# Storing split weight blocks of the input projection for their later uses, in a hybrid decoder layer

## The chip, the cores and the metric

The kernel runs on one core of a Trainium2 chip. The metric is device time in microseconds (us) of one execution; it is the median of several runs, 1899.0 us before the change. Five engines work side by side, each on its own queue in order: TensorE (PE; its weight loads are listed apart as PEld), VectorE (DVE), ScalarE (ACT), GpSimd (POOL) and SyncE (SP), which here issues nearly all transfers between HBM and the on-chip memory (SBUF). TensorE writes into PSUM banks.

## The reference

One decoder layer, 2048 tokens, width 1024, all in float32:

```
hn  = RMSNorm(x)
[u | q | k | v] = hn @ W_in          # W_in: 1024 x 2048, four parts of 512 columns
y_pool = per group of 128 columns: (mean of the last w tokens - own value) @ pool_w, times pool_scale   # w = 2, 4, 8, 16
y_attn = strictly causal stick-breaking attention, 8 heads of 64
h = x + concat(RMSNorm(y_pool), RMSNorm(y_attn)) @ W_out
h = h + relu(RMSNorm(h) @ W_up)**2 @ W_down
y = RMSNorm(h)
```

## The kernel before, in words

*Number format.* Every float32 operand of a large product is split into a high part (rounded to the type float32r) and a low part (the rest). A product is three matmuls: high by high, high by low, low by high. The split is the helper `split`: ScalarE copies the high part (line 145), VectorE subtracts it from the source (line 146). These two lines thus carry the splits of many tiles, and the tile names in the profile tell them apart: `hl` is a weight granule, `h` a normalised activation, `qk` and `vt` query, key and value tiles, `at` the attention weights, `pls` a pooled tile, `mix` a normalised mixer output.

*Tiling.* The 2048 tokens are four token blocks of 512 (j = 0 to 3). W_in is 16 column blocks of 128 (0 to 3 pool groups, 4 to 7 queries, 8 to 11 keys, 12 to 15 values). One block of W_in against one token block is a step: 8 chunks of the inner dimension, each three matmuls of 128 x 512 (lines 177, 178, 179), 24 in all, into one PSUM tile `pd`.

*Weights.* A column block is loaded raw (`load_raw`, line 159, 512 KB, two buffers `raw`), and split into two granules of four chunks each (`weights`). A granule `hl` holds its high and low parts, 512 KB in all. Five buffers `hl` rotate (WAHEAD = 5): a granule's buffer is free when TensorE has done the matmuls of the granule five back. `weights` is called ahead of each step and readies granules up to five ahead of it.

*Order of the steps.* `front(0)` runs ten steps of token block 0 (blocks 4, 8, 5, 9, 12, 13 and then pool groups 0 to 3), then a shared stage in which blocks 6, 10, 14, 7, 11, 15 are each split once and used for token blocks 0 and 1, then the ten blocks of token block 1. `front(1)` does the same for token blocks 2 and 3. The ten blocks that are not shared are thus loaded and split four times each, once per token block. In the trace the stages lie at 0 to 67 us (token block 0), 67 to 162 (shared, 0 and 1), 162 to 238 (token block 1), 238 to 318 (token block 2), 318 to 413 (shared, 2 and 3) and 413 to 494 (token block 3). Then come 32 steps with W_out (`tail`, to 692 us), and the feed-forward part to the end.

*Work around the steps.* After a step its PSUM tile is evacuated: `keep_qk` splits queries and keys and stores them to HBM, `keep_v` does so for values over a transpose (`ptv`), `pool_group` forms the pooled tile (`pl`), splits it (`pls`) and multiplies it by pool_w into `pp` (lines 396 to 398). The attention of earlier tokens (`near`) is a generator of pieces put between the steps by due times (`advance`, RATIO_FRONT). Norms are pieces in a list `later`, taken one or two per step (`catch_up`). `inv_rms` makes a root chain: sums of squares by matmuls into `pm` (line 204), a first VectorE step (line 212), ten and more small GpSimd steps, then matmuls into `pr` (line 230) that spread the result, which ScalarE copies (line 250). At the start of the last stage `load_mix` (line 547) brings the mixer's tiles `h<-mx` for W_out.

*Queues.* The program states an order and some constraints (`issue_after`): among them, `catch_up` (line 1491) holds the pieces in `later` behind the newest weight split on ScalarE's or VectorE's queue (`last_split`), and `load_x` (line 304) holds the loads of x behind the newest raw load (`last_load`). The order on each engine's queue is then chosen by a planner that simulates the times of all instructions. Each queue, SP's too, runs in the order chosen: an instruction that waits holds up those behind it.

*Names.* The change touches `load_raw`, `weights`, `start`, `in_proj`, the list `wlist` of column blocks in the order of their first use, and the call for W_out in `tail`. It uses the lists EARLY (4, 8, 12, 5, 9, 13) and POOL (0, 1, 2, 3).

Of the kernel before, what the change touches and what calls it, by code (L numbers as in the profile page):

```python
# [8 lines left out]
F32 = mybir.dt.float32  # L9
F32R = mybir.dt.float32r  # L10
# [5 lines left out]
P = 128  # L16
# [9 lines left out]
G = 4  # L26
# [15 lines left out]
POOL, EARLY, FIRST = (0, 1, 2, 3), (4, 8, 12, 5, 9, 13), (4, 8, 5, 9, 12, 13)  # L42
# [3 lines left out]
def hymba_block(ctx: ExitStack, tc: tile.TileContext, xT, gains, w_in, pool_w, w_out, w_up, w_down, out):  # L46
    nc = tc.nc
# [5 lines left out]
    dram = pool("dram", 1, space=bass.MemoryType.DRAM)  # L53
# [76 lines left out]
    os_ = [dram.tile([H // 2, P, T], F32, name=f"os{j}") for j in range(NT)]  # L130
    mx = [[dram.tile([P, 2, T], F32R, name=f"mx{j}_{k}") for k in range(KD)] for j in range(NT)]
    hs = [dram.tile([KD, P, T], F32, name=f"hs{j}") for j in range(NT)]

    su = [[[dram.tile([P, 2, T], F32, name=f"su{q}_{i}_{c}") for c in range(2)] for i in range(7)] for q in range(2)]
    sd = [[[dram.tile([P, 2, T], F32, name=f"sd{q}_{i}_{c}") for c in range(8)] for i in range(7)] for q in range(2)]
# [6 lines left out]
    def split(dst, src):  # L142

        hi, lo = dst
        nc.scalar.activation(hi, src, AF.Copy)  # L145
        return nc.vector.tensor_tensor(lo, src, hi.bitcast(F32), ALU.subtract)  # L146
# [6 lines left out]
    raws, grans, last_split, last_mm, last_load = [], [], [None], [None], [None]  # L153
    done = [None, None]

    def load_raw(i):
        while len(raws) <= min(i, len(wlist) - 1):
            raw = wp.tile([P, 2, G, P], F32, tag="raw", name="raw")
            last_load[0] = nc.sync.dma_start(raw, wlist[len(raws)].rearrange("p (x k) c -> p x k c", x=2))
            raws.append(raw)  # L160

    def weights(first, n):

        for i in range(len(grans), min(first + WAHEAD, 2 * len(wlist))):
            load_raw(i // 2)
            hl = wp.tile([P, 2, G, P], F32R, tag="hl", name="hl", align_bytes=256, bufs=WAHEAD)
            last_split[0] = split((hl[:, 0], hl[:, 1]), raws[i // 2][:, i % 2])
            grans.append(hl)
            load_raw(i // 2 + 1)
        return grans[first:first + n]  # L170

    def products(ps, hls, acts, half_behind=None):
# [112 lines left out]


    wlist = []
    prog = []

    def step(n, emit, again=False):  # L290
        prog.append((n, emit, again))
# [15 lines left out]
    def start():  # L307

        xt = st[0]["x"] = x0p.tile([P, KD, T], F32, tag="big", name="xt")
        for _ in range(2):  # L310
            raws.append(wp.tile([P, 2, G, P], F32, tag="raw", name="raw"))
        def weight(c, x):
            nc.sync.dma_start(raws[c][:, x], wlist[c][:, x * G:(x + 1) * G])

        nc.scalar.dma_start(xt[:, 0], xT[0, :, 0])
        weight(0, 0)
        nc.sync.dma_start(gt, gains)
        weight(1, 0)
        for k in range(1, KD):
            if k == 3:  # L320
                weight(0, 1)
            if k == 4:
                weight(1, 1)
            nc.sync.dma_start(xt[:, k], xT[0, :, k])

        zb = zero.bitcast(BF16)
        pz = psx.tile([P, T], F32, tag="px", name="pzero")
        for i in range(WARM):
            nc.tensor.matmul(pz, zb[:, 0:P], zb[:, 0:T], start=True, stop=True)
# [41 lines left out]
    def pool_group(j, g, ps):  # L371
        w = WINDOWS[g]
        if g == 0:
            st[j]["y"] = pa.tile([P, 4, T], F32, tag="yb", name="yb", bufs=1)
        u = pa.tile([P, PAD + T], F32, tag="u", name="u")
        nc.gpsimd.tensor_copy(u[:, 0:PAD], carry[:, g])
        if j == 0:
            took = nc.vector.tensor_tensor(u[:, PAD:], ps, st[0]["r"], ALU.mult)
        else:
            took = nc.scalar.activation(u[:, PAD:], ps, AF.Copy)  # L380
        nc.gpsimd.tensor_copy(carry[:, g], u[:, T:T + PAD])
        cur, lag = u, 1
        while lag < w:
            nxt = pa.tile([P, PAD + T], F32, tag="s", name="s")
            lo = 2 * lag - 1
            nc.vector.tensor_tensor(nxt[:, lo:], cur[:, lo:], cur[:, lo - lag:PAD + T - lag], ALU.add)
            cur, lag = nxt, 2 * lag
        pl = pa.tile([P, T], F32, tag="ev", name="pl")
        nc.vector.scalar_tensor_tensor(pl, cur[:, PAD:], 1.0 / w, u[:, PAD:], op0=ALU.mult, op1=ALU.subtract)
        if j == 0:  # L390
            nc.vector.tensor_tensor(pl[:, 0:w - 1], cur[:, PAD:PAD + w - 1], recip[:, 0:w - 1], ALU.mult)
            nc.vector.tensor_tensor(pl[:, 0:w - 1], pl[:, 0:w - 1], u[:, PAD:PAD + w - 1], ALU.subtract)
        d = pa.tile([P, 2, T], F32R, tag="st", name="pls", align_bytes=256, bufs=3)
        split((d[:, 0], d[:, 1]), pl)
        pp = psx.tile([P, T], F32, tag="px", name="pp")
        nc.tensor.matmul(pp, pw[0][:, 0, g], d[:, 0], start=True, stop=False)
        nc.tensor.matmul(pp, pw[0][:, 0, g], d[:, 1], start=False, stop=False)
        nc.tensor.matmul(pp, pw[0][:, 1, g], d[:, 0], start=False, stop=True)
        nc.scalar.activation(st[j]["y"][:, g], pp, AF.Copy, scale=gs[:, g:g + 1])
        return took  # L400
# [46 lines left out]

    def in_proj(j, c, again=False):
        if not again:
            wlist.append(w_in[c])  # L450
        if c < 4:
            evac = lambda ps: pool_group(j, c, ps)
        elif c < 12:
            evac = lambda ps: keep_qk(j, c % 4, qs if c < 8 else ks, ps)
        else:
            evac = lambda ps: keep_v(j, c - 12, ps)
        n = sum(1 for _ in prog if _[0]) if j == 0 else None

        def emit(w):
            dense(j, "h", w, evac, None, "pm" if n == 2 else None)  # L460

        def emit_two(w):

            ps = [psd.tile([P, T], F32, tag="pd", name="pd") for _ in range(2)]
            for k, (hi, lo) in enumerate(st[0]["h"]):
                for i in range(2):
                    hl, c = w[2 * i + k // G], k % G
                    nc.tensor.matmul(ps[i], hl[:, 0, c], hi, start=(k == 0), stop=False)
                    nc.tensor.matmul(ps[i], hl[:, 0, c], lo, start=False, stop=False)
                    last_mm[0] = nc.tensor.matmul(ps[i], hl[:, 1, c], hi, start=False, stop=(k == KD - 1))  # L470
            for i in range(2):
                done[:] = [done[1], pending[i](ps[i])]

        if n is not None and len(pending) < 2:
            pending.append(evac)
            if len(pending) == 2:
                step(4, emit_two)
            return
        step(2, emit, again)
# [9 lines left out]
    def drained(j):  # L489
        while j not in finished:  # L490
            state["due"] = 0.0
            advance(0.1)
# [62 lines left out]
    def tail(first):  # L555

        def root(j):

            if not (first and j < 2):
                drained(j)  # L560
                st[j]["todo"] = attn_norm(j, lambda: make_h(j))

        def mixes(j):
            load_mix(j, KD if first and j < 2 else 4)
            if "todo" in st[j]:
                st[j]["amix"] = st[j].pop("todo")()

        def begin(j):
            catch_up(len(later))
            st[j]["m"] += st[j].pop("amix", [])  # L570
            if j > 0:
                norm2(j - 1)
            if j == 2:
                sums_first()

        if first:
            note(to_out)
        else:
            note(lambda: (root(0), mixes(0), load_acc(0)))
        for j in range(NT):  # L580
            if j == 2 and first:
                note(to_last)
            note(lambda j=j: begin(j))
            for c in range(KD):
                if c == 0 and j == 0 and not first:
                    note(lambda: root(1))
                if c == 0 and j + 1 < NT:
                    note(lambda j=j: mixes(j + 1))
                if c == (2 if j == 0 else 4) and j + 2 < NT:
                    note(lambda j=j: root(j + 2))  # L590
                if c == 0 and j == 2:
                    note(lambda j=j: load_acc(j))
                if c == 4 and j in (0, 2):
                    note(lambda j=j: load_acc(j + 1))
                if c == 3 and j == NT - 1:
                    note(begin_ffn)
                wlist.append(w_out[c])
                step(2, lambda w, j=j, c=c: dense(j, "m", w, lambda ps: add_acc(j, c, ps)))


# [1042 lines left out]
```

## Time and profile before

| | us |
|---|---|
| runs shown | 1898.85, 1899.0, 1906.92 (median 1899.0) |
| profiled execution, its own time | 1905.2 |
| its span, first to last instruction | 1903.5 |
| TensorE busy | 1869.5 |
| VectorE busy | 1480.9 |
| ScalarE busy | 1023.7 |
| weight splits, 168: ScalarE, VectorE | 104.2, 113.9 |
| bytes moved | 535.91 MB, mean 282 GB/s |

A row that names an engine, a line and `out<-in` is a group of equal instructions; after `|` stand their busy time and the mean time of one in ns, then the idle time of the engine ahead of them with what ended most of it. A row that begins with a stretch (from:to, in us from the span's start) gives the stretch's length, each engine's busy time in it with its count of instructions, the clock granted to TensorE as a share, the share of time for which the 16 DMA engines were busy, and GB/s. A row `A <- B` gives who waited for whom: us in all, how often, the longest. TensorE's matmuls overlap, so busy time counts a matmul until its modelled end.

### The profile page before, as it was taken

What the parts mean: (1) busy time and instruction counts of PE and PEld (TensorE: products, weight loads), DVE (VectorE), ACT (ScalarE), POOL (GpSimd) and SP (SyncE); (2) the same over time, 40 slices, a digit from 0 to 9 for tenths busy, and PEclk for the clock granted to TensorE, in tenths of its full rate; (3) what the DMA queues carried; (4) which work ended last, traced back from release to release, by engine and by line L of the source; (5) the groups of instructions that cost most, each with busy time, mean ns of one, the idle gap of its engine ahead of it and who ended that gap; (6) DMA issues with size and microseconds to landing.
All of it is one profiled execution on the core that took longest, in us unless ns stands there. A gap on an engine that the chain in (4) does not pass through costs nothing.

```text
span 1903.5 us, 26682 instructions
## 1 busy us (share of the span) xinstructions
PE 1869.5 (98%) x8883; PEld 1555.5 (82%) x8883; DVE 1480.9 (78%) x2151; ACT 1023.7 (54%) x1616; POOL 242.1 (13%) x463
## 2 busy tenths in 40 slices
PE   9999999999999999999999999999999999999997
PEld 7888788888888888778888888887788888888886
DVE  6887799668866976778699988786566677888774
ACT  5565466555544465554557555554332665656543
POOL 0333233223421050000000000000010010020120
PEclk9999999999999999999999999999999999999998
DMA  6686696798788867887899888889999899999752
GB/s 224 204 269 196 191 308 213 239 322 278 272 316 306 296 229 254 284 306 276 286 365 334 313 300 278 301 284 326 378 311 326 289 322 301 334 297 342 290 210 91
DMA packets 222164, 535.91 MB, mean 282 GB/s; under 512 B 26048, under 2 KB 32192, under 8 KB 218176
## 3 DMA queue, kind: packets, MB, share of 16 engines
q1 hardware_dynamic: 217264, 525.46, 79.2%
q0 software_dynamic: 4608, 8.39, 2.4%
q8 instruction: 72, 1.18, 0.3%
q14 instruction: 76, 0.62, 0.1%
q10 hardware_dynamic: 144, 0.26, 0.0%
HBM read 349.46 MB, written 184.55 MB: 281 GB/s over the span
## 4 chain that ended last, share of the span: by engine, by line
PE 45%; DMA 6%; DVE 4%; issue 2%; ACT 1%; POOL 0%; SPq 0%; DVEq 0%; ACTq 0%
PE pb L1274 14%; PE pb L1451 12%; PE pY L1101 10%; PE pZ L1101 5%; PE pX L1101 2%; DMA ar<-sd 1%; DVE hw L146 1%; DMA ar<-sdi 1%; PE pb L1391 1%; DMA t<-in_w_down_dram 1%; DMA su<-hs 0%; DMA sd<-a 0%; DMA td<-t 0%; DMA sdi<-a 0%; DMA b<-in_w_down_dram 0%
## 5 line engine op out<-in xcount | busy, mean ns | idle before, releaser
L1101 PE MATMUL pY<-sa,hw 128*128 128x512 f32 x1536 | 366.3, 389 | 3.0 <-ACT u L1024 2.6
L1101 PEld LDWEIGHTS pY<-sa,hw 128*128 128x128 f32 x1536 | 288.0, 188 | 64.3 <-ACT u L1024 3.9
L1274 PE MATMUL pb<-ad,wd 128*128 128x512 f32 x1344 | 305.1, 389 | 0.3 <-DVE ad L146 0.3
L177 PE MATMUL pd<-h,hl 128*128 128x512 f32 x752 | 299.0, 398 | 3.5 <-DVE acc L813 2.0
L179 PE MATMUL pd<-h,hl 128*128 128x512 f32 x752 | 297.6, 396 | 0.0
L178 PE MATMUL pd<-h,hl 128*128 128x512 f32 x752 | 297.5, 396 | 0.0
L1274 PEld LDWEIGHTS pb<-ad,wd 128*128 128x128 f32 x1344 | 252.2, 188 | 53.1 <-DVE ad L146 0.7
L1451 PE MATMUL pb<-ad,wd 128*128 128x512 f32 x1104 | 253.9, 390 | 2.4 <-ACT ad L145 2.0
L1451 PEld LDWEIGHTS pb<-ad,wd 128*128 128x128 f32 x1104 | 206.5, 188 | 46.1 <-ACT ad L145 2.4
L146 DVE TENSOR_TENSOR ad<-ar,ad 128x1024 fp32r<-128x1024 f32 x160 | 193.9, 1220 | 44.6 <-ACT ad L145 44.2
L145 ACT ACTIVATE ad<-ar 128x1024 fp32r<-128x1024 f32 x160 | 168.2, 1053 | 95.2 <-PE pb L1451 32.0
L1101 PE MATMUL pZ<-sa,hw 128*128 128x512 f32 x768 | 187.0, 390 | 1.1 <-DVE a L1044 1.0
L1101 PEld LDWEIGHTS pZ<-sa,hw 128*128 128x128 f32 x768 | 143.7, 188 | 32.4 <-DVE a L1044 2.6
L177 PEld LDWEIGHTS pd<-h,hl 128*128 128x128 f32 x752 | 142.6, 190 | 31.8 <-issue 2.8
L145 ACT ACTIVATE hl<-raw 128x512 fp32r<-128x512 f32 x168 | 104.2, 631 | 116.2 <-PE pd L179 66.1
L179 PEld LDWEIGHTS pd<-h,hl 128*128 128x128 f32 x752 | 142.5, 189 | 28.2
L178 PEld LDWEIGHTS pd<-h,hl 128*128 128x128 f32 x752 | 142.5, 190 | 26.8
L146 DVE TENSOR_TENSOR hl<-raw,hl 128x512 fp32r<-128x512 f32 x168 | 113.9, 684 | 45.8 <-ACT hl L145 45.5
L1018 ACT ACTIVATE a<-a 128x512 f32<-128x512 f32 x96 | 60.1, 629 | 97.4 <-DVE a L1060 43.0
L146 DVE TENSOR_TENSOR hw<-rt,hw 128x512 fp32r<-128x512 f32 x128 | 86.3, 683 | 26.0 <-ACT hw L145 26.0
L145 ACT ACTIVATE wd<-wq 128x1024 fp32r<-128x1024 f32 x56 | 59.3, 1060 | 76.8 <-PE pb L1274 68.1
L146 DVE TENSOR_TENSOR wd<-wq,wd 128x1024 fp32r<-128x1024 f32 x56 | 68.4, 1221 | 34.2 <-ACT wd L145 34.2
(218 smaller groups left out, 2736.2 us busy)
## 6 DMA issues: line engine op xcount, KB each, us to landing
ar<-sd SPq DMA_DIRECT2D x96, 512.0 KB, 5.7
ar<-sdi SPq DMA_DIRECT2D x64, 512.0 KB, 5.8
rb<-in_w_up_dram SPq DMA_DIRECT2D x30, 1024.0 KB, 6.6
sd<-a SPq DMA_DIRECT2D x104, 256.0 KB, 5.1
raw<-in_w_in_dram SPq DMA_DIRECT2D x50, 512.0 KB, 4.8
sdi<-hr SPq DMA_DIRECT2D x96, 256.0 KB, 5.5
wr<-in_w_down_dram SPq DMA_DIRECT2D x48, 512.0 KB, 5.6
sd<-s SPq DMA_DIRECT2D x88, 256.0 KB, 4.7
```

Of the source, the lines that this page charges most:

```text
L145: nc.scalar.activation(hi, src, AF.Copy)
L146: return nc.vector.tensor_tensor(lo, src, hi.bitcast(F32), ALU.subtract)
L177: nc.tensor.matmul(ps, hl[:, 0, c], hi, start=(k == 0), stop=False)
L178: nc.tensor.matmul(ps, hl[:, 0, c], lo, start=False, stop=False)
L179: mm = nc.tensor.matmul(ps, hl[:, 1, c], hi, start=False, stop=(k == n - 1))
L1018: nc.scalar.activation(t, src, AF.Relu)
L1101: nc.tensor.matmul(t, w[:, wx, c], a[:, ax, c % 2], start=first and c == 0 and x == 0, stop=last and c == G - 1 and x == 2, skip_group_che ...
L1274: nc.tensor.matmul(b, t[:, wx, 2 * (kk % 2) + c, i * P:(i + 1) * P], a[:, ax, c], start=p in ("P1", "P5", "P2") and kk == 0 and c == 0 and ...
L1391: nc.tensor.matmul(b[:, cols], block(t, wx, c, n), a[:, ax, c, cols], start=False, stop=(i == 1 and c == 1 and x == 2), skip_group_check=True)
L1451: nc.tensor.matmul(ps[q, n], block(t, wx, c, n), left_[q][:, ax, c], start=(n_ in ("P1", "P3") and kk == 0 and c == 0 and x == 0), stop=(n ...
```

## The change

The ten blocks in EARLY and POOL get two HBM buffers each, one for a split granule. When such a block is split for the first time (token block 0, use "keep"), each granule is also stored there, 20 stores of 512 KB. At its three later uses (use "split", token blocks 1, 2 and 3) there is no raw load and no split: each granule is loaded from HBM straight into its `hl` buffer, 60 loads of 512 KB in place of 30 raw loads of 512 KB and 60 splits. The six shared blocks and W_out are loaded raw and split as before (use "raw"). A split load sets neither `last_split` nor `last_load`. Every entry of `wlist` now carries the block, its use and its buffers.

```diff
+    ws = {c: [dram.tile([P, 2, G, P], F32R, name=f"ws{c}_{x}") for x in range(2)] for c in EARLY + POOL}
...
     def load_raw(i):
         while len(raws) <= min(i, len(wlist) - 1):
+            if wlist[len(raws)][1] == "split":
+                raws.append(None)
+                continue
             raw = wp.tile([P, 2, G, P], F32, tag="raw", name="raw")
-            last_load[0] = nc.sync.dma_start(raw, wlist[len(raws)].rearrange("p (x k) c -> p x k c", x=2))
+            last_load[0] = nc.sync.dma_start(raw, wlist[len(raws)][0].rearrange("p (x k) c -> p x k c", x=2))
             raws.append(raw)

     def weights(first, n):
         for i in range(len(grans), min(first + WAHEAD, 2 * len(wlist))):
             load_raw(i // 2)
             hl = wp.tile([P, 2, G, P], F32R, tag="hl", name="hl", align_bytes=256, bufs=WAHEAD)
-            last_split[0] = split((hl[:, 0], hl[:, 1]), raws[i // 2][:, i % 2])
+            use, kept = wlist[i // 2][1:]
+            if use == "split":
+                nc.sync.dma_start(hl.bitcast(F32), kept[i % 2].bitcast(F32))
+            else:
+                last_split[0] = split((hl[:, 0], hl[:, 1]), raws[i // 2][:, i % 2])
             grans.append(hl)
             load_raw(i // 2 + 1)
+            if use == "keep":
+                nc.sync.dma_start(kept[i % 2].bitcast(F32), hl.bitcast(F32))
         return grans[first:first + n]
...
     def in_proj(j, c, again=False):
         if not again:
-            wlist.append(w_in[c])
+            use = "raw" if c not in ws else "split" if c in used else "keep"
+            used.add(c)
+            wlist.append((w_in[c], use, ws.get(c)))
...
-                wlist.append(w_out[c])
+                wlist.append((w_out[c], "raw", None))
```

More of the change, by code (lines that the diff above doesn't have):

```diff
@@ L287, in hymba_block @@
     wlist = []
+    used = set()
     prog = []
@@ L312, in weight @@
         def weight(c, x):
-            nc.sync.dma_start(raws[c][:, x], wlist[c][:, x * G:(x + 1) * G])
+            nc.sync.dma_start(raws[c][:, x], wlist[c][0][:, x * G:(x + 1) * G])
         nc.scalar.dma_start(xt[:, 0], xT[0, :, 0])
```

## The prediction

> **What bounds the kernel now.** I read the page first, then busy time by stage, then TensorE's own waits, then the order of work around its largest gaps.
>
> ```profile
> span 1903.5 us, 26682 instructions
> PE 1869.5 (98%) x8883; PEld 1555.5 (82%) x8883; DVE 1480.9 (78%) x2151; ACT 1023.7 (54%) x1616; POOL 242.1 (13%) x463
> L145 ACT ACTIVATE hl<-raw 128x512 fp32r<-128x512 f32 x168 | 104.2, 631 | 116.2 <-PE pd L179 66.1
> L146 DVE TENSOR_TENSOR hl<-raw,hl 128x512 fp32r<-128x512 f32 x168 | 113.9, 684 | 45.8 <-ACT hl L145 45.5
> ```
>
> TensorE works 98% of the span; 34.0 us are left (1903.5 - 1869.5). The change removes no matmul, so whatever it wins is inside those 34 us or in a clock that was granted low. ScalarE's and VectorE's splits matter only where TensorE waits for these engines. The stages that hold the reused blocks (token block 1, 2, the second shared stage, token block 3) show how much that is:
>
> ```profile
> core 0: us, PE busy (x) PEld busy (x) DVE busy (x) ACT busy (x) POOL busy (x), PEclk, DMA share, GB/s
> 0.00:67.00 67.00, 63.69 (x282) 49.81 (x283) 49.79 (x114) 36.67 (x62) 9.66 (x29) 1.00 0.76 248
> ...
> 162.00:238.00 76.00, 72.70 (x366) 60.95 (x364) 54.47 (x89) 39.87 (x74) 20.80 (x46) 0.96 0.54 169
> 238.00:318.00 80.00, 79.21 (x463) 68.32 (x463) 75.73 (x112) 55.71 (x105) 27.05 (x47) 1.00 0.87 278
> 318.00:413.00 95.00, 92.66 (x523) 78.09 (x521) 73.98 (x107) 53.47 (x97) 29.42 (x61) 1.00 0.76 247
> 413.00:494.00 81.00, 79.03 (x431) 67.58 (x430) 61.89 (x91) 47.51 (x88) 26.56 (x41) 0.96 0.90 297
> ...
> 200.00:210.00 10.00, 6.70 (x35) 5.39 (x34) 9.58 (x16) 5.81 (x11) 2.84 (x3) 0.88 0.71 221
> 210.00:220.00 10.00, 10.00 (x36) 7.99 (x36) 5.35 (x12) 4.05 (x8) 0.00 (x0) 0.78 0.62 159
> 450.00:460.00 10.00, 8.03 (x42) 6.83 (x41) 7.60 (x12) 5.08 (x10) 6.72 (x16) 0.84 0.89 280
> 460.00:470.00 10.00, 10.00 (x47) 8.30 (x47) 7.41 (x11) 5.04 (x10) 1.15 (x2) 0.82 0.58 153
> ```
>
> Idle TensorE by stage is 76 - 72.70 = 3.30, 80 - 79.21 = 0.79, 95 - 92.66 = 2.34 and 81 - 79.03 = 1.97 us: 8.4 in all. The granted clock (the column before the DMA share) falls twice, right after the two largest gaps: 10 x (0.12 + 0.22) = 3.4 us of clock lost at 200-220, and 10 x (0.16 + 0.18) = 3.4 us at 450-470. The ceiling of this change on the profiled execution is therefore 8.4 + 6.8 = 15.2 us, 0.8%.
>
> TensorE's own waits at those places (engine and line, what it waited for, us, times, longest):
>
> ```profile
> PE pp L396 <- ACT pls L145: 2.1, 1, 2.1
> PE pp L397 <- DVE pls L146: 1.2, 1, 1.2
> PE pr L230 <- POOL yr L240: 1.7, 1, 1.7
> PE pr L230 <- POOL yr L241: 0.3, 1, 0.3
> PE pd L177 <- DVE qk L146: 0.8, 1, 0.8
> ```
>
> The first two are a pool group of token block 1, the next two a root chain in token block 3, the last a projection in token block 2 that waits for a PSUM bank.
>
> **The change part by part.** *Removed.* Ten blocks, three later uses, two granules each: 60 splits, 60 x 0.631 = 37.9 us of ScalarE and 60 x 0.684 = 41.0 us of VectorE. Most of it runs beneath TensorE and is worth nothing. It is worth something where a split stands in VectorE's queue ahead of what TensorE waits for. VectorE before the first gap, and ScalarE, VectorE and the root chain before the second:
>
> ```profile
> 198.67 0.68 DVE L146 TENSOR_TENSOR hl<-raw,hl 128x512 fp32r<-128x512 f32 x1
> ...
> 201.01 0.69 DVE L146 TENSOR_TENSOR hl<-raw,hl 128x512 fp32r<-128x512 f32 x1
> ...
> 202.22 0.68 DVE L146 TENSOR_TENSOR hl<-raw,hl 128x512 fp32r<-128x512 f32 x1
> ...
> 203.93 0.69 DVE L146 TENSOR_TENSOR hl<-raw,hl 128x512 fp32r<-128x512 f32 x1 [0.42 <-ACT hl L145]
> 204.54 0.69 DVE L389 SCALAR_TENSOR_TENSOR pl<-s,u 128x512 f32<-128x512 f32 x1
> ...
> 445.69 0.95 PE L204 MATMUL pm<-inv,ss 128*128 128x1 f32 x8
> 446.90 1.16 ACT L145 ACTIVATE hl<-raw 128x512 fp32r<-128x512 f32 x2 [4.04 <-DMA raw<-in_w_in_dram]
> 447.56 1.29 DVE L146 TENSOR_TENSOR hl<-raw,hl 128x512 fp32r<-128x512 f32 x2 [1.18 <-ACT hl L145]
> 448.78 0.15 DVE L212 TENSOR_SCALAR v<-pm 128x4 f32<-128x4 f32 x1
> ```
>
> First gap: four splits, each holding the queue 0.6 us (203.93 to 204.54), and 0.42 us of waiting for ScalarE's half lie ahead of the pooled tile: 4 x 0.6 + 0.4 = 2.8 us. Without them 3.3 - 2.8 = 0.5 us of gap is left, and with it, I take it, no fall of the clock: 2.8 + 3.4 = 6.2 us. Second gap: the sums (pm) were ready at 445.69 + 0.95 = 446.64, and VectorE reached the root's first step at 448.78, since two splits stood ahead and these waited for a raw load. That is 2.1 us, more than the 1.97 us gap: 1.97 + 3.4 = 5.4 us. The 0.8 us wait for qk sits in a stage where VectorE is 75.73 of 80 us busy; 20 x 0.684 = 13.7 us leave it, and I count it all. In the shared stage the blocks stay raw; its 2.34 us I leave. Sum of gains: 6.2 + 5.4 + 0.8 = 12.4 us.
>
> The Trainium skill ("TensorE: Matmul & The Clock Gate", Part 1) lets the clock fall after an idle window of about 3.4 us. No single gap here is so long; rows that lose clock after 2.1 + 1.2 and after 1.7 + 0.3 us of idling do not agree with it as a threshold on one gap. By that rule closing these gaps would not bring the clock back, and the gain would be 12.4 - 6.8 = 5.6 us.
>
> *Added: stores.* 20 stores of 512 KB (0.524 MB) in the first stage. The nearest rows are issues, with size and median time to landing:
>
> ```profile
> raw<-in_w_in_dram SPq DMA_DIRECT2D x50, 512.0 KB, 4.8
> mx<-mix SPq DMA_DIRECT2D x24, 512.0 KB, 4.7
> h<-mx SPq DMA_DIRECT2D x24, 512.0 KB, 8.5
> ```
> One raw load's issue on SP (ns, shortest, median, longest), and two stretches, an empty one and a full one:
> ```profile
> L159 SPq DMA_DIRECT2D raw<-in_w_in_dram x50: 327/338/703, 10.6 to 459.7; - x50
> ```
> ```profile
> 70.00:80.00 10.00, 9.30 (x41) 7.23 (x41) 10.00 (x18) 5.78 (x9) 0.00 (x0) 1.00 0.01 2
> 410.00:420.00 10.00, 10.00 (x59) 8.45 (x58) 4.67 (x8) 4.34 (x8) 0.00 (x0) 1.00 1.03 412
> ```
>
> The first 67 us moved 67 x 0.248 = 16.6 MB; 20 x 0.524 = 10.5 more make 27.1 MB, which at the 412 GB/s of a full stretch take 66 us. So the DMA engines become full there and spill into 70-80, which is empty (2 GB/s). A store is off TensorE's path: it lands in 4.7 us (mx), while the buffer it reads comes round again only five granules later. I take 0; the bound above is one late raw block, a gap like the largest, 3.3 us; a gain is excluded, since nothing is taken from this stage.
>
> *Moved: loads.* 30 raw loads of 512 KB go, 60 split loads of 512 KB come: 15.7 MB more, and with the stores 26.2 MB on 535.91. SP issues 60 + 20 - 30 = 50 more transfers at 0.338 us, 17 us spread over 490. Capacity holds: token block 3 moved 81 x 0.297 = 24.1 MB, with 20 x 0.262 = 5.2 more 29.3 MB, or 71 us at 412 GB/s in 81; token block 2 22.2 + 5.2 = 27.4 MB, 67 us in 80.
>
> What gets shorter is the lead. A raw block waits for a split, and stands two blocks ahead. A split load must wait until TensorE is done with the granule five back, so it leads by four granules: 4 x 81 / 20 = 16 us. Behind it in SP's order stand stores of q, k, v and loads for the attention. The rows for what such a wait costs (SP's waits at the raw load, and the fullest stretch):
>
> ```profile
> SPq L159 <- DVE hl L146: 128.3, 46, 8.4
> ```
> ```profile
> 413.00:433.00 20.00, 20.00 (x106) 16.88 (x105) 8.96 (x13) 9.19 (x18) 0.41 (x1) 1.00 1.03 370
> ```
> ```profile
> raw<-in_w_in_dram SPq DMA_DIRECT2D x2, 512.0 KB, 5.1
> ```
>
> The SP waits were 128.3 / 46 = 2.8 us in the mean and 8.4 at most, and TensorE lost nothing to them. At 413-433, the stretch of the last two rows, the engines are full with the mixer's tiles and two raw loads. Five granules in 20 us need 5 x 0.524 = 2.6 MB in place of 1.0: 1.6 MB / 370 GB/s = 4.3 us behind. Wait 2.8 + landing 8.5 + backlog 4.3 = 15.6 us against 16: just in time. Late loads cost between 0 and, at the longest wait, 8.4 + 8.5 + 4.3 - 16 = 5.2 us; I take 1.2, nearer to nothing, since the mean wait fits.
>
> *Order.* Two constraints loosen, since a split load sets neither anchor: the pieces in `later` (norms, roots) were held behind the newest weight split, x of token block 2 behind the newest raw load; in the three stages both anchors are now those of the shared blocks before. And the planner writes the order on every queue anew. The trace prices neither; the bounds are one gap like the largest with its clock, 6.7 us, won or lost. I take 0, for nothing tells the sign.
>
> Sum: 1905.2 (the profiled execution; its span and 1.7 us around it) - 12.4 + 1.2 = 1894.0 us. The median shown is 1899.0, 6.2 us under the profiled one, and one run is 1906.9; a gap with its fall of clock is 6.7 us, so I take it that some executions lack one already. Against the median the forecast is thus only -5 us, -0.3%. A difference under 0.5% (9.5 us) cannot be told from none here.
>
> **The rivals.**
> *All of it goes, and the next stage gains too.* The 15.2 us of the ceiling, and the 1.8 us that TensorE waits later for VectorE's accumulation:
>
> ```profile
> PE pd L177 <- DVE acc L813: 2.0, 2, 1.8
> ```
>
> 1905.2 - 15.2 - 1.8 = 1888.2. For it speaks VectorE's load; against it that this and the shared stage's 2.34 us lie where raw blocks are still split.
>
> *The gaps are not the splits'.* TensorE comes to pool group or root as early as before and waits for the next thing in VectorE's queue (between 204.54 and the group's second split stand an addition, a half of the attention and a scan), or the clock falls as before. Gaps half kept and clock lost: 1905.2 - 2.8 - 2.0 - 0.8 + 1.2 = 1900.8. For it speaks that TensorE was ready for both. It is also what the skill's rule on the clock, above, would come to.
>
> *Loads come late (slower).* Place: the full stretches of token blocks 2 and 3. It decides from the point where SP's wait and the landing pass 16 us. Then each granule there is late by some 0.9 us (backlog 4.3, landing 8.5, and a wait of 4.1, between the mean and the longest), ten of the 40 granules make 9 us, and two pauses that lower the clock cost 6.8: 1894 + 15.8 = 1910. For it speaks the share of 1.03 in the last stage's first 20 us; against it 0.54 in token block 1. The skill's "DMA: Bandwidth & Descriptors" (Specifications) gives about 358 GB/s as one core's share of HBM; by it token block 3 would need 29.3 / 0.358 = 82 us and be bound by transfers. The row with 412 GB/s does not agree.
>
> **How the numbers follow.** Forecast 1894: 0.45. Everything gone, 1888: 0.12. Gaps stay, 1901: 0.25. Late loads, 1910: 0.18. Faster by over 0.5% is under 1889.5: the second case and 0.10 of the first (the planner's gap to the good), 0.22. Slower is over 1908.5: late loads and 0.02 more, 0.20. Within: 0.58. The range reaches from the second case less the planner's half, 1884, to the late loads plus as much, 1914; the forecast's own is 1887 to 1901.
>
> **What would show it.** In the changed profile the hl splits should count 108, not 168; VectorE and ScalarE should lose about 41 and 38 us; DMA should move about 562 MB. Right: no wait of pp for pls above 1 us in token block 1, no wait of pr for the root in block 3, granted clock 1.00 at both places. Wrong: waits of the projection's matmuls (pd) for a DMA into hl, landing of these loads over 9 us, or the same two falls of the clock; and TensorE's 34 us of idling unchanged.

## The result, and the profile after

The change made the kernel slower: 1.0046 times the time before, 95% interval 1.0027 to 1.0066. The means are 1914.1 us (ten executions) and 1905.3 us (nine; a tenth, of 3806.7 us, has no part in the ratio), so 8.8 us are lost. The medians of all ten each are 1913.4 and 1907.4 us. The profiled execution of the changed kernel has a span of 1914.2 us, against 1903.5.

The page of the changed kernel (line numbers are up by 10 to 13: 177 to 179 became 187 to 189, 145 became 146, `raw` is loaded at 163, `hl` at 173, and stored at 179):

```profile
span 1914.2 us, 26625 instructions
PE 1873.5 (98%) x8883; PEld 1556.8 (81%) x8883; DVE 1446.9 (76%) x2091; ACT 990.3 (52%) x1556; POOL 233.5 (12%) x463
...
DMA packets 229363, 562.12 MB, mean 294 GB/s; under 512 B 26848, under 2 KB 32992, under 8 KB 225376
...
L146 ACT ACTIVATE hl<-raw 128x512 fp32r<-128x512 f32 x108 | 65.7, 628 | 77.3 <-PE pd L189 33.3
...
hl<-ws SPq DMA_DIRECT2D x60, 512.0 KB, 5.6
```

The change does what it says: 108 splits in place of 168, 562 MB. The rows of the splits lose 41 us on VectorE and 38.5 us on ScalarE, as forecast; the busy time of the two engines falls by 34 and 33 us. TensorE idles 40.7 us in place of 34.0.

To see where the time went I cut both executions at the end of the last projection matmul of each stage. Lengths in us, with the difference from before in brackets. Attention pieces move between neighbouring stages, so token block 2 and the shared stage behind it are best read together.

```
                 token 0      shared 0,1   token 1      token 2      shared 2,3   token 3      W_out         feed-forward
before           67.2         94.3         74.9         78.1         97.1         80.5         198.9         1212.3
after            75.5 (+8.3)  97.5 (+3.2)  68.2 (-6.8)  86.7 (+8.5)  91.5 (-5.6)  79.0 (-1.5)  199.5 (+0.6)  1216.3 (+4.0)
```

Token block 1 gains what was forecast. Token block 0 and the shared stage behind it lose 11.5 us, token block 2 with its shared stage 2.9. The feed-forward part lies 4.0 us apart although VectorE, ScalarE, GpSimd and SP run the same instructions in the same order there (between 720 and 1870 us of the trace before: 1205, 877 and 77 instructions, and 954 transfers issued by SP). Of the 4.0 us, 1.7 are clock: TensorE is granted 0.83 at 1310 to 1320 us in the changed kernel, and 1.00 in the same part before. Single executions of the kernels below have 1209.5 to 1220.2 us there. No experiment explains these 4 us, and I do not put them down to the change.

TensorE's waits in the changed kernel, over the whole span:

```profile
PE pd L187 <- ACT hl L146: 4.6, 2, 3.4
PE pd L187 <- DVE qk L147: 3.7, 1, 3.7
...
PE po L688 <- issue: 2.5, 1, 2.5
PE pz L629 <- ACT sg L637: 2.0, 1, 2.0
PE ptv L451 <- DVE vf L446: 1.6, 1, 1.6
...
PE pd L187 <- DMA hl<-ws: 0.7, 1, 0.7
```

The waits of token block 1 (pp for pls) and of the root in token block 3 (pr for yr) are gone. The first new wait is for a weight split in token block 0, the second for a query tile in token block 2; a split load is late by only 0.7 us. Four of these places also lose clock:

```profile
50.00:60.00 10.00, 9.63 (x42) 8.13 (x43) 4.69 (x8) 3.19 (x6) 2.43 (x7) 0.83 1.01 365
120.00:130.00 10.00, 9.27 (x38) 7.61 (x39) 7.42 (x13) 4.69 (x10) 0.00 (x0) 0.83 0.61 183
260.00:270.00 10.00, 6.33 (x20) 5.02 (x19) 5.10 (x8) 3.51 (x7) 1.15 (x2) 0.66 1.00 339
430.00:440.00 10.00, 7.91 (x38) 6.68 (x39) 3.62 (x5) 3.74 (x7) 0.80 (x2) 0.83 1.03 333
```

The wait in token block 0, followed back. Before, SP issues five raw loads in a row and only then the stores of queries; after, the raw load stands behind them and behind a store of split weights. SP's rows before:

```profile
19.18 16.77 SPq L159 DMA_DIRECT2D raw<-in_w_in_dram  x5
39.36 2.43 SPq L428 DMA_DIRECT2D qs<-qk  x4
```

SP, ScalarE, VectorE and TensorE after:

```profile
32.20 0.60 ACT L260 ACTIVATE r<-pr 128x512 f32<-128x512 f32 x1 [6.06 <-PE pr L240]
32.69 1.14 ACT L146 ACTIVATE hl<-raw 128x512 fp32r<-128x512 f32 x2
34.03 1.28 DVE L147 TENSOR_TENSOR hl<-raw,hl 128x512 fp32r<-128x512 f32 x2
...
34.74 0.32 SPq L179 DMA_DIRECT2D ws<-hl  x1
35.16 2.44 SPq L439 DMA_DIRECT2D qs<-qk  x4
...
42.79 0.59 SPq L179 DMA_DIRECT2D ws<-hl  x1
43.42 0.45 SPq L163 DMA_DIRECT2D raw<-in_w_in_dram  x1
...
49.69 1.15 ACT L146 ACTIVATE hl<-raw 128x512 fp32r<-128x512 f32 x2 [3.11 <-DMA raw<-in_w_in_dram]
50.37 0.80 PE L187 MATMUL pd<-h,hl 128*128 128x512 f32 x1 [3.42 <-ACT hl L146]
```

The raw buffer came free at 34.03 + 1.28 = 35.3, and the load that needed it was issued at 43.4: 8.1 us in the queue. It landed some 6.3 us later. The buffer itself also came free late: on ScalarE the planner now puts the root's result (r, at 32.20) ahead of the splits, and from 22 to 32 us no split runs there. Before, six splits ran ahead of it from 24.85 us on:

```profile
24.85 1.94 ACT L145 ACTIVATE hl<-raw 128x512 fp32r<-128x512 f32 x3 [1.23 <-DMA raw<-in_w_in_dram]
...
34.24 0.63 ACT L145 ACTIVATE hl<-raw 128x512 fp32r<-128x512 f32 x1 [2.09 <-PE pd L179]
37.35 0.60 ACT L250 ACTIVATE r<-pr 128x512 f32<-128x512 f32 x1 [2.47 <-PE pr L230]
```

Whether it is the bytes, the waits on SP or the order that costs is what the first experiments ask.

### The profile page after: what moved, and what is told of

It reads as the page before. It is cut to its first block, busy times and chain, and to the rows that moved or that the text cites. A ratio compares the mean times of both kernels' runs of the same rounds, so it can differ in the third digit from the quotient of the medians.

```text
span 1914.2 us, 26625 instructions
## 1 busy us (share of the span) xinstructions
PE 1873.5 (98%) x8883; PEld 1556.8 (81%) x8883; DVE 1446.9 (76%) x2091; ACT 990.3 (52%) x1556; POOL 233.5 (12%) x463
## 4 chain that ended last, share of the span: by engine, by line
PE 50%; DVE 3%; DMA 3%; ACT 1%; issue 1%; POOL 0%; SPq 0%; DVEq 0%; ACTq 0%
PE pb L1287 16%; PE pY L1114 12%; PE pb L1464 12%; PE pZ L1114 6%; PE pX L1114 3%; DMA hn<-hs 1%; DVE hw L147 1%; DMA sdi<-a 1%; PE pb L1404 1%; DMA ar<-sd 0%; DMA t<-in_w_down_dram 0%; DMA sdi<-hr 0%; DMA hr<-sd 0%; ACT a L1031 0%; ACT hw L146 0%
## 5 line engine op out<-in xcount | busy, mean ns | idle before, releaser
L1114 PEld LDWEIGHTS pZ<-sa,hw 128*128 128x128 f32 x768 | 144.1, 188 | 35.5 <-DVE a L1057 5.6
L146 ACT ACTIVATE hl<-raw 128x512 fp32r<-128x512 f32 x108 | 65.7, 628 | 77.3 <-PE pd L189 33.3
L146 ACT ACTIVATE wd<-wq 128x1024 fp32r<-128x1024 f32 x56 | 59.4, 1061 | 78.1 <-PE pb L1287 67.8
L1114 PE MATMUL pX<-sa,hw 128*128 128x512 f32 x384 | 93.3, 389 | 0.0
```

The lines of the kernel that those rows point to most:

```text
L1114: nc.tensor.matmul(t, w[:, wx, c], a[:, ax, c % 2], start=first and c == 0 and x == 0, stop=last and c == G - 1 and x == 2, skip_group_che ...
```

## The experiments

Theories at the start: *stores* (the 20 stores cost, in token block 0), *loads* (the split loads cost, by their shorter lead or their bytes), *order* (the two loosened anchors cost). The first three kernels each do one part alone. Each ratio below is to executions of the kernel before that were made together with that kernel's. Stage lengths are those of one profiled execution each.

**Stores alone.**

```diff
-            use = "raw" if c not in ws else "split" if c in used else "keep"
+            use = "raw" if c not in ws or c in used else "keep"
```

> The 20 stores of token block 0 alone; the three later uses load raw and split as before (same result). Theory 'stores': the loss is made in token block 0, where the stores stand on SP ahead of raw loads; the end of token block 0 moves from 67 to about 75 us and the time to +8 to +11 us (ratio about 1.005). Theory 'loads': nothing happens here, ratio 1.000, since the cost lies in the shorter lead of the split loads. Theory 'order': anchors are as in the kernel before, ratio 1.000.

Measured 1.0068 (1.0050 to 1.0086), 13 us. Token block 0 takes 76.0 us (+8.8), the shared stage 98.7 (+4.4); every stage behind is within 1.2 us of before. The waits of token block 0 are those of the changed kernel:

```profile
PE pd L187 <- ACT hl L146: 4.4, 2, 3.2
```

**Loads alone.**

```diff
-            use = "raw" if c not in ws else "split" if c in used else "keep"
+            use = "raw" if c not in ws or (c not in used and c != 4) else "split" if c in used else "keep"
...
-            wlist.append((w_in[c], use, ws.get(c)))
+            wlist.append((w_in[c], use, ws.get(c) and ws[4]))
```

> The 60 split loads with 2 stores in place of 20: all later uses load the two granules of block 4, so that the later uses compute with other weights (work, traffic and waits are those of the change). Theory 'stores': without them the gain of the removed splits is left, -3 to -8 us (ratio 0.997), the pool group's wait in token block 1 gone. Theory 'loads': token block 2 loses about 8 us as in the changed kernel, ratio 1.002 to 1.004. Theory 'order': as the changed kernel, 1.004.

Measured 1.0009 (0.9997 to 1.0021). Token block 1: 68.2 us (-6.8), just as in the changed kernel. Token block 2 with its shared stage: -1.0; W_out +4.6. So the loads give back what they gain, most of it in W_out and not in token block 2, where *loads* had put it; the result lies between the two theories.

**Anchors alone.** The three later uses of the ten blocks keep their raw loads and splits; only `last_split` and `last_load` stay where they were.

```diff
-            last_split[0] = split((hl[:, 0], hl[:, 1]), raws[i // 2][:, i % 2])
+            done_split = split((hl[:, 0], hl[:, 1]), raws[i // 2][:, i % 2])
+            if use == "raw":          # "free" at the later uses of the ten blocks
+                last_split[0] = done_split
... (the same for last_load)
```

> The kernel before, with all its splits and raw loads and no transfer added; only the two anchors are not moved on by the three later uses of the ten blocks, as in the change. Theory 'order': the pieces of norms slide to worse places, +4 to +9 us (ratio 1.002 to 1.005). Theories 'stores' and 'loads': within 3 us of before, ratio 1.000.

Measured 0.9974 (0.9962 to 0.9985): a gain of 4 to 5 us. The two anchors fall as a cause of the loss. The gain is small amounts in token block 3 (-1.6), W_out (-1.0) and the two stages ahead (-0.5 together). This version is faster than both kernels.

**Stores issued by GpSimd.**

```diff
-                nc.sync.dma_start(kept[i % 2].bitcast(F32), hl.bitcast(F32))
+                nc.gpsimd.dma_start(kept[i % 2].bitcast(F32), hl.bitcast(F32))
```

> The whole change with the 20 stores issued by GpSimd instead of SP. If the stores cost by their place in SP's order (a raw load stands behind a store that waits for its split), token block 0 ends near 68 us again and the time falls by 6 to 9 us under the changed kernel (ratio 0.999 to before). If they cost by filling the DMA engines, token block 0 ends at about 75 us as in the changed kernel and the ratio stays at 1.004.

Measured 1.0098 (1.0082 to 1.0115), worse than the changed kernel: token block 0 takes 79.0 us. It does not tell the two readings (place on SP, bytes) apart, since the stores now stand in GpSimd's queue with the root chain, and TensorE waits 5.2 us for the root's result at 58 us.

**Small stores.** The kernel with the stores alone, with the same 20 issues and an eighth of the bytes.

```diff
-                nc.sync.dma_start(kept[i % 2].bitcast(F32), hl.bitcast(F32))
+                nc.sync.dma_start(kept[i % 2][:, 0, 0].bitcast(F32), hl[:, 0, 0].bitcast(F32))
... (later uses raw, as in the run with the stores alone)
```

> The 20 stores of token block 0 alone, each of 64 KB in place of 512 KB (only the first chunk's high part is stored; nothing reads it, so the result is the same). Same count of issues and same waits on SP as with the full stores. If the issues and waits on SP's queue are what costs, token block 0 and the shared stage behind it still lose 10 us or more, ratio 1.005 to 1.007. If the bytes are (full DMA engines, or a planner that reckons with them), both stages are within 2 us of before, ratio 1.000 to 1.001.

Measured 1.0013 (0.9998 to 1.0028); token block 0 takes 66.9 us, the shared stage 95.8 (+1.5). So 20 issues on SP do not cost by themselves. But the order changed with the bytes too: with small stores seven splits run ahead of the root's result from 25 us on, with full stores none.

**Late stores.** Each store is stated three granules later.

```diff
-            if use == "keep":
-                nc.sync.dma_start(kept[i % 2].bitcast(F32), hl.bitcast(F32))
+            if i >= 3 and wlist[(i - 3) // 2][1] == "keep":
+                nc.sync.dma_start(wlist[(i - 3) // 2][2][(i - 3) % 2].bitcast(F32), grans[i - 3].bitcast(F32))
```

> The 20 full stores alone, each stated three granules later in the program, behind the raw loads that come next. If the stores cost by standing ahead of the raw loads on SP, the loss of 13 us shrinks to 3 us or less, ratio 1.001. If the bytes cost, it stays above 8 us, ratio 1.004 to 1.007.

Measured 1.0045 (1.0030 to 1.0060), the profiled execution with token block 0 at 74.0 and the shared stage at 97.3 us. This kernel also kept the split loads (its later uses are those of the change, not raw ones as the text above has it), so its 1.0045 stands beside the changed kernel's 1.0046, and its +9.7 us in the two stages beside +11.5. Stating the stores later does nothing for the raw loads: the planner still puts stores of q and k ahead of them.

**Stored in token block 1.**

```diff
-            use = "raw" if c not in ws else "split" if c in used else "keep"
-            used.add(c)
+            use = "raw" if c not in ws or j == 0 else "keep" if j == 1 else "split"
```

> The blocks are stored in token block 1 (DMA engines 0.54 busy there) in place of token block 0, and loaded split in token blocks 2 and 3 alone. Theory 'stores cost where the DMA engines and the raw loads are tight': token block 0 as before, token block 1 within 2 us of before, then the loads' own effect as with loads alone (+4.6 and -5.6 us in the two stages behind), ratio 0.998 to 1.001. A theory by which each stored byte costs wherever it stands: token block 1 loses 8 us or more, ratio 1.004.

Measured 1.0059 (1.0038 to 1.0080). Token block 1 costs nothing more (74.7 us, -0.2) with the DMA engines at 0.91 in place of 0.54:

```profile
162.00:238.00 76.00, 73.24 (x367) 60.70 (x366) 52.15 (x85) 38.49 (x71) 19.60 (x46) 0.96 0.91 317
```

So stored bytes do not cost by themselves. The time is lost in token block 2 with its shared stage (+1.2) and in W_out (+10.3, with a 5.0 us wait for sums of squares at 563 us and a granted clock of 0.66 at 560 to 570), and the gap of token block 1 stays, since its splits stay. The expectation of 1.001 at most was wrong, and no run shows why W_out, where weights are loaded raw as before, loses so much here.

**Two blocks.** Blocks 4 and 8 alone are stored, and loaded split in token block 1 alone; the rest as with the anchors alone.

```diff
-    ws = {... for c in EARLY + POOL}
+    ws = {... for c in FIRST[:2]}
... (anchors as in the run with the anchors alone)
-            use = "raw" if c not in ws else "split" if c in used else "keep"
+            use = "raw" if c not in EARLY + POOL else "keep" if c in ws and j == 0 else "split" if c in ws and j == 1 else "free" if c in used else "raw"
```

> Blocks 4 and 8 alone are stored (4 stores in place of 20) and loaded split in token block 1 alone, where their splits stood ahead of the pool group that TensorE waited for; all other later uses are raw, with the anchors left as in the run with the anchors alone. If the gap of token block 1 is worth its 3.3 us and the clock 3.4, and four stores cost nothing: token block 1 at 68 us, ratio 0.994. If the gap only moves: as the anchors alone, 0.997.

Measured 0.9988 (0.9974 to 1.0001). Token block 1 gains 5.2 us, but the shared stage ahead of it loses 5.5 to new waits at 82 to 84 us (for a normalised activation and an attention load, 2.5 us) with a fall of the clock (0.66 at 80 to 90). Token block 0 loses 2.0. Four stores suffice to change the plan there.

**Raw loads first, stores alone, and in the whole change.**

```diff
-            last_load[0] = nc.sync.dma_start(raw, ...)
+            with tc.high_priority():
+                last_load[0] = nc.sync.dma_start(raw, ...)
```

> The 20 full stores alone, with the raw loads given priority in the planner, so that a raw load is put on SP as soon as its buffer is free, ahead of stores of q and k. If the cost of the stores is the place of the raw loads behind other work on SP, token block 0 and the shared stage lose 4 us or less in place of 13, ratio 1.001 to 1.002. If it is the full DMA engines (a raw load lands later wherever it stands), they lose 8 us or more, ratio 1.004 to 1.007.

> The whole change with the same priority for raw loads. If SP's order was the cost: 6 to 9 us under the changed kernel, ratio 0.999 to before. If the bytes are: as the changed kernel, 1.004.

Measured 1.0039 (1.0026 to 1.0052) and 1.0037 (1.0023 to 1.0051). Token block 0 falls from 76.0 and 75.5 to 71.4 us in both: half of its loss was the place of the raw loads. The first raw load behind the root's result is now issued at 35.5 us, as soon as its buffer is free, but on ScalarE the result still stands ahead of the splits (no split from 22 to 32 us). The shared stage stays at 98.7 and 99.9.

**Loads alone with four `st` buffers.** In token block 2 of the changed kernel ScalarE waits, ahead of the query tile, for a mixer store to land, because the three buffers `st` that mixer, query, value and pooled tiles share are in flight. First mixer stores' landing before (238 to 268 us), then rows of the changed kernel:

```profile
DMA to landing us min/median/max: 4.2/4.3/5.3
```

```profile
DMA to landing us min/median/max: 5.9/6.4/7.5
...
256.90 0.63 ACT L146 ACTIVATE mix<-nt 128x512 fp32r<-128x512 f32 x1 [3.46 <-DMA mx<-mix]
...
263.73 0.80 PE L187 MATMUL pd<-h,hl 128*128 128x512 f32 x1 [3.67 <-DVE qk L147]
```

The DMA engines are hardly fuller in this stretch than before (share 1.00 against 0.99 at 238 to 268 us). What differs is what is under way when SP issues a mixer store. In the changed kernel it is seven transfers each time, one or two of them split loads of 512 KB; before, it is four to seven, most of them small attention loads.

```diff
-        d = pa.tile([P, 2, T], F32R, tag="st", name="qk", align_bytes=256, bufs=3)
+        d = pa.tile([P, 2, T], F32R, tag="st", name="qk", align_bytes=256, bufs=4)
... (the same for mix, pls and vt)
```

> The run with the split loads alone (2 stores, later uses with block 4's weights), with four buffers in place of three for the tiles that are stored after their split (st: mixer outputs, q, k, v, pooled tiles). Theory: in token block 2 ScalarE waits for a mixer store to land (landing 6.4 us with the fuller engines, 4.3 before) because all three buffers are in flight, and TensorE behind it; with four, TensorE's wait for qk at the start of token block 2 (1.8 us with the loads alone, 3.7 in the changed kernel) falls under 0.8 us and the ratio from 1.001 to 0.998. Rival, the loads themselves come late: nothing changes, 1.001.

Measured 0.9978 (0.9966 to 0.9991). The wait for qk goes (1.8 to none in token block 2), as does W_out's loss (+4.6 to +0.1). With stores and buffers out of the way the kernel with the loads gains. The landing of the mixer stores does not get shorter (6.7 us in the median): the fourth buffer takes the wait for it away. Most of what is left at TensorE is late loads:

```profile
PE pd L187 <- DMA hl<-ws: 4.4, 2, 3.9
```

**All remedies.** Raw loads first, four `st` buffers, and the loads of x for token block 1 stated one step later.

```diff
-            if q == 0 and i == 2:
+            if q == 0 and i == 3:
```

> The whole change with priority for raw loads, the loads of x for token block 1 stated one step later, and four st buffers. If the two costs found (raw loads behind in token block 0, stores in flight in token block 2) are all there is, the change is left with its gain: ratio 0.994 to 0.997. If the bytes cost in any order, 1.001 or more.

Measured 1.0008 (0.9997 to 1.0019), some 7 us (0.0038 of 1907) under the changed kernel. Token block 0 is back at 68.2 us with every store still there (the last is issued at 67.1 us):

```profile
0.00:68.00 68.00, 64.90 (x292) 50.90 (x293) 49.31 (x111) 36.68 (x63) 9.03 (x31) 1.00 0.94 344
```

The DMA engines are as full as in the changed kernel (0.94 and 0.93) and 1 us is lost in place of 8: in token block 0 it is the order, not the bytes as such. On ScalarE four splits from 26 us on run ahead of the root's result again:

```profile
26.23 1.16 ACT L146 ACTIVATE hl<-raw 128x512 fp32r<-128x512 f32 x2 [4.70 <-DMA raw<-in_w_in_dram]
30.21 1.16 ACT L146 ACTIVATE hl<-raw 128x512 fp32r<-128x512 f32 x2 [2.83 <-DMA raw<-in_w_in_dram]
...
35.06 0.60 ACT L261 ACTIVATE r<-pr 128x512 f32<-128x512 f32 x1 [1.32 <-PE pr L241]
```

This run adds two things to raw loads first, x later and the fourth buffer, and no run has x later without the buffer. The buffer alone does not mend token block 0 (78.1 us in the changed kernel with it, below). The shared stage keeps its +4.3, and token block 3 a wait of 3.4 us for a split load.

Three of the last four kernels have the fourth `st` buffer alone (`bufs=3` made 4 on mix, pls, qk and vt, as above): put on the kernel before, on the changed kernel, and on the kernel with the anchors alone.

> The kernel before with four st buffers, nothing else. If the fourth buffer only helps where the change makes stores land late: ratio 0.999 to 1.001, and the pool group's wait in token block 1 stays. If the buffer is a gain of its own: 0.997 or less, and the gain of the loads with four buffers (0.998) is not the loads'.

Measured 0.9999 (0.9985 to 1.0013): the fourth buffer alone is worth nothing, so the 0.9978 above is not the buffer's.

> The changed kernel with four st buffers. If the wait for qk in token block 2 hangs on them, it falls from 3.7 us under 0.8, the clock stays up there, and the ratio to before falls from 1.0046 to about 1.002; the loss of token block 0 stays. If not, 1.0046.

Measured 1.0048 (1.0029 to 1.0067). The wait for qk is gone and with it the fall of the clock there; token block 2 with its shared stage loses nothing any more (-2.4). Yet the ratio is the same. In the profiled execution (1921.5 us, the longest of the six) token block 3 is 3.7 us longer than in the changed kernel, with a late load:

```profile
PE pd L187 <- DMA hl<-ws: 4.5, 1, 4.5
```

In the changed kernel the same granule landed no earlier (432.6 us, against 433.3 here), but TensorE had stood for 2.5 us just before (ahead of the attention product po, without a releaser in the profile), which covered the lateness; here that wait is 0.3 us. The rest is not this trade: token block 0 and the shared stage behind it are another 3.7 us longer than in the changed kernel, and W_out is 7.1 us longer with a wait of 3.4 us for sums of squares, which no run explains.

> The run with the anchors alone (0.9974) and four st buffers: the candidate to beat both kernels. If the two are independent and the buffer is worth nothing by itself, 0.997; if it is worth something, 0.995.

Measured 0.9998 (0.9984 to 1.0011): two harmless edits, 0.9974 and 0.9999 alone, make 0.9998 together. The gain of the anchors is one of order that another edit takes away again; it is not a property of the anchors. This run is also the nearest comparison for the loads with four buffers, which loosen the same anchors: 0.9978 (0.9966 to 0.9991) against 0.9998. The two intervals touch, so a gain of the loads is likely rather than certain.

**Mixer tiles later.** All remedies, and `load_mix(0, KD)` stated with a later note:

```diff
-        note(lambda: (..., (load_acc(0), load_mix(0, KD), attn_norm(1)) if q else norm1(b + 1), pace(1)))
+        note(lambda: (..., (load_acc(0), attn_norm(1)) if q else norm1(b + 1), pace(1)))
...
-                note(lambda: (catch_up(len(later)), pace(1)))
+                note(lambda: (catch_up(len(later)), load_mix(0, KD), pace(1)))
```

> The change with all the remedies of the run before (ratio 1.0008), and the loads of the mixer's tiles for W_out stated six steps later, behind the first blocks of token block 3. If TensorE's wait there is a split load landing late behind 4 MB of mixer tiles, it goes (3.5 us, and 1.7 of clock), ratio 0.998. If the load is late for another reason, the wait stays and the ratio too.

Measured 1.0002 (0.9989 to 1.0016). The wait stays:

```profile
PE pd L188 <- DMA hl<-ws: 5.0, 4, 3.2
```

So it is not the mixer tiles' place alone. When the late granules' buffers came free, when SP issued their loads, and when TensorE first used them, from the traces (us; granules counted from 0 in the order of use: 87 is the second half of token block 3's second block, 88 and 89 are its third block):

```
                 granule   free    issued   used
changed kernel   87        415.5   424.3    432.7
                 88        419.8   431.6    438.7
                 89        422.5   436.6    442.0
loads, st 4      87        398.9   408.2    417.2
                 88        403.2   417.2    422.6
mixer later      88        410.1   418.4    426.0
                 89        412.9   422.4    432.2
```

Each of these loads spends 8 to 14 us in SP's queue after its buffer is free. In the program every transfer waits for the one eight before it to land (in the traces none of SP's is issued sooner), so with full engines SP issues no faster than they drain. SP's waits in the last kernel, 400 to 440 us:

```profile
SPq L440 <- DMA h<-mx: 2.4, 3, 0.9
SPq L456 <- DMA h<-mx: 1.7, 2, 0.9
...
SPq L174 <- DMA hl<-ws: 1.0, 1, 1.0
```

## Why the prediction was wrong

*Removed splits: the first gap right, the second not shown.* The first gap was put at 6.2 us, and token block 1 gained 6.8 in every kernel that loads all its ten blocks split, with the clock at 1.00 there. The second was put at 5.4 us: its wait is gone, but token block 3 gained 1.5, since a new wait of 2.5 us (the profile names no releaser) with 1.7 us of clock came in its place. Nor does that gap need the splits gone. Three kernels that keep all splits in token block 3 run it in 76.7 to 77.1 us (small stores, stores alone with raw loads first, kernel before with four buffers), with 1.3 to 1.8 us of waiting for the root and the clock at 1.00; the kernels with split loads take 78.8 to 82.7. The 0.8 us for qk, "I count it all", became 3.7.

*Added stores: the step that failed.* "A store is off TensorE's path ... I take 0", with one gap of 3.3 us as the bound. The stores alone cost 13 us, and the changed kernel loses 11.5 us in the same two stages. I had worked out that the DMA engines would fill, and looked for the harm at the buffer that a store reads. It is done to the next raw load, in two ways. On SP the planner put that load behind stores of q and k: with raw loads first token block 0 falls from 75.5 to 71.4 us. On ScalarE it put the root's result ahead of the splits, so that the raw buffers came free late: in the run with all remedies splits run ahead of it again and token block 0 takes 68.2 us, with the same 20 stores. The first way is shown by a run of its own, the second by a run that also changes a buffer. For the shared stage's 3 to 4 us the runs show only that they shrink with small stores (+1.5), are gone with stores issued by GpSimd (94.2 us), and stay with all remedies; their cause is open.

*Moved loads: mechanism right, size off, and one link missing.* The wait ahead of a load was taken from the mean at the raw load, 2.8 us; for the granules of token block 3 above it was 8 to 14. By the sum it was 15.6 us from a free buffer to the landing, just inside the lead of 16. In the changed kernel the three granules above landed 17.1, 18.9 and 19.5 us after (at 432.6, 438.7 and 442.0 us). TensorE shows only 0.7 us of this because it had stood for po just before (2.5 us, and 1.7 us of clock); in five other kernels the longest wait for a split load in this stage is 3.2 to 4.5 us. The link I did not have is the mixer's store: with split loads under way ahead of it, it lands in 6.4 us in place of 4.3, ScalarE waits for its buffer, and TensorE behind it for 3.7 us and 3.4 us of clock. That the buffer is what TensorE waits for is shown by the runs with a fourth one; why the landing is longer is read from the traces alone.

*Order: bounds right.* 6.7 us either way was allowed; the anchors alone gave -4 to -5, and with the fourth buffer nothing.

*Base.* From three runs I took it that executions at 1899 lack a gap; no profile shows that. The nine comparable executions have a median of 1906.9 and a mean of 1905.3 us, close to the profiled 1905.2. The sum, -12.4 + 1.2 us, was thus a forecast of faster by 0.6%, where 0.5% slower was measured.

*Rivals.* "Loads come late" had the sign and, at 1910, nearly the time, but not the place: it was given to the loads, at 0.18, and most of the loss is the stores'. "The gaps are not the splits'" fell in token block 1; for token block 3 it was nearer than the forecast. The 358 GB/s of the Trainium skill ("DMA: Bandwidth & Descriptors", Specifications) did not bind here either: the row of 50 to 60 us above has 365 GB/s. The Trainium skill's threshold for the clock ("TensorE: Matmul & The Clock Gate", Part 1, about 3.4 us) disagrees with this trace again: a wait of 1.6 us (ptv for vf) is followed by 0.83 at 120 to 130 us. Nor does the length of one wait decide it here: the clock stays at 1.00 behind a wait of 2.0 us (pz for sg) at 89 us.

## What to carry to other kernels

Where TensorE is 98% busy, cost a store by what it pushes back in the issuing queue and in the planned order of the other engines, not only by the buffer that it reads. When loads are made to depend on a rotating buffer, price their lead in the fullest stretch, with the queue's wait of that stretch, and follow who else waits for a landing there. A wait that is removed can uncover the next, so look at what took its place before calling a remedy useless.

## What was not expected of the hardware

In token block 0 twenty stores of 512 KB cost 8 us in one order and 1 us in another, with the DMA engines 0.93 busy in the first and 0.94 in the second; the stage behind keeps its loss in both. And edits that change no work moved the time by -0.26% (anchors), while two such edits together moved it by nothing; with executions of one kernel 11 us apart (nine of the kernel before: 1898.9 to 1909.8), an effect under 0.3% needs the interval and not the profile of one execution. W_out, whose own steps the change leaves as they were, lies 1.0 us under to 10.3 us over its time before in the kernels above.
